# Moving one query projection ahead of the attention stage, shifting a pair of heads, and splitting norms into smaller steps in a one-core encoder layer

## The chip, the cores and the metric

One core of a Trainium2 chip runs the whole program. The metric is the device time of one execution in microseconds (us), smaller is better, as the median of several runs. Engines are named as in the profile: PE is TensorE's matmuls, PEld its weight loads, DVE is VectorE, ACT is ScalarE, POOL is GpSimd, SP is SyncE, which issues the DMAs.

## The reference, cut to what matters

One encoder layer over 1024 prompt frames and 32 sample frames of width 1024, all in float32:

```python
h = adaln_in(x, gains[0], sh1, sc1)
x = x + FFN_RES * g1[:, None] * rmsnorm(swiglu(h, w1_gate, w1_up, w1_down), gains[1])
h = adaln_in(x, gains[2], sh2, sc2)
qa, ka, va, qb, kb, vb = jnp.split(h @ w_in, SPLITS, axis=-1)
oa, ob, rows = mixers(qa, ka, va, qb, kb, vb)
o = jnp.concatenate([rmsnorm(oa, group_gains[:WIDTH_A]), rmsnorm(ob, group_gains[WIDTH_A:])], axis=-1) @ w_out
x = x + g2[:, None] * rmsnorm(o, gains[3])
h = adaln_in(x, gains[4], sh3, sc3)
x = x + FFN_RES * g3[:, None] * rmsnorm(swiglu(h, w2_gate, w2_up, w2_down), gains[5])
```

Mixer A is chunked attention with 8 heads over up to 576 keys; mixer B has 8 query heads on 2 key heads, a window of 128, and a learned sink per head. Both have relative biases. The new key and value rows are outputs too.

## The kernel before

**Tiling.** Activations lie transposed (features on the partitions), in three blocks of frames, `TB`: 384, 384 and 288 wide, the last one holding the 32 sample frames. A product with a weight is kept exact to float32 by splitting both sides into a high and a low part: `mm3` (L324 to L327) does three matmuls for each of the 8 slices k of the features: weight high times input high, weight high times input low, weight low times input high. `split_w` (L299) loads one weight column block of 512 KB by a DMA into a `raw` tile (3 buffers), rounds it on ACT into the high part (L303) and subtracts on DVE for the low part (L304), in a tile of `wpool` (8 buffers).

**Stages.** The first feed-forward part (`ffn` with key h1), then projections and attention, then the output product `wo` with its norms, then the second feed-forward part (key h3). Norms run aside: `step(n)` advances the generators in the list `side`, first one first. A norm squares and sums on ACT, POOL and DVE, takes the sums of the partitions by PE (`pss`, L357), computes the root on a dozen small DVE operations (L334 to L338), spreads it by PE (`pr`, L405), and scales: `norm_h` writes `h_hi` (ACT, L440 or L444) and `h_lo` (DVE or POOL, L446, L449). Between sums and spread `mean_rstd` lets `waits[0]` steps pass.

**Around the attention.** For each block tb the loop at L1077 waits for the block's norm (`need(("h2", tb))`), then projects mixer B's keys and values (`kv_piece`, tile `pv`), the queries of mixer B's first pair (`q0_piece`, tile `pq`), and mixer A's first values. Then 72 attention tiles n run: 36 of mixer B (four pairs of one sample tile and 8 tiles i each), 18 of mixer A's pairs 0 and 1, and from n = 54 on those of pairs 2 and 3, sorted by i + LAG * (p - 2). Each tile is scores (`S`, `Sb`, `Ss`), softmax on DVE and ACT, transposes (`pp`, `ppb`, `pps`), and products with the values (`po`).

**Fill.** The projections that later tiles need run between the tiles. `STAGES` says from which tile to which a list of units is spread; `fill(rate)` takes from it, twice a tile, what the costs in `COST` allow. `prepare` gets a pair's bias and cached keys three tiles ahead. From n = 67 on one piece of the output product (`out_piece`, tile `wo`, 24 matmuls) goes in per tile; the other 19 follow the loop, with six steps of the norms behind each. `group_norm(tb, g)` norms one block of mixer A (g = 0) or B (g = 1) ahead of them.

**Order.** What is written is a priority. When the program is built, a list scheduler with its own timeline picks for each engine, among the instructions whose inputs and buffers it believes ready, the one that is written first. On the chip each engine then runs its list in that order. Some projections are seen between the last `dn` matmuls of the feed-forward part for that reason.

The parameters that the change touches: OUTSTEP, STAGES, LAG, and the order of the matmuls in `up` inside `ffn` (L540).

Of the kernel before, what the change touches and what calls it, by code (L numbers as in the profile page):

```python
# [8 lines left out]
F32R = mybir.dt.float32r  # L9
# [8 lines left out]
KT = D // 128  # L18
# [16 lines left out]

PACE = 2
FAST = 10
OUTSTEP = 6
ABREAST = 1
POOL_ADDS = (1, 2)  # L40
GN1 = 55
# [21 lines left out]
LEAD_B = 2  # L63
MANUAL = False
WAIT = 3
PREP = 3
STAGES = ((0, 34), (37, 54))
RATE = 1.0
OUTS = (0,) * 13 + (1,) * 5
LAG = 0.5  # L70
KEEP = [(5, 6, 7), None, None]


# [1 line left out]
def encoder_step(ctx: ExitStack, tc, x_prompt, x_sample, cache_a_k, cache_a_v, cache_b_k, cache_b_v,  # L75
# [220 lines left out]
        return bs  # L296


    def split_w(src):  # L299
        r = rpool.tile([128, 8, 128], F32, name="raw", tag="r")  # L300
        dma.dma_start(r, src)
        w = wpool.tile([128, 2, 8, 128], F32R, name="w", tag="w")
        ae.activation(w[:, 0], r, AF.Copy)  # L303
        ve.tensor_sub(w[:, 1], r, w[:, 0])  # L304
        return w

    def split_cols(wm, c):
        return split_w(wm[0, :, 128 * c:128 * c + 128].rearrange("(k p) n -> p k n", p=128))

    def split_rows(wm, r):  # L310
        return split_w(wm[0, 128 * r:128 * r + 128, :].rearrange("p (k n) -> p k n", n=128))
# [12 lines left out]
    def mm3(ps, w, k, hi, lo, start, stop):  # L324
        te.matmul(ps, w[:, 0, k], hi, start=start, stop=False)  # L325
        te.matmul(ps, w[:, 0, k], lo, start=False, stop=False)  # L326
        te.matmul(ps, w[:, 1, k], hi, start=False, stop=stop)  # L327


    def rsqrt(v, n, m):  # L330
# [170 lines left out]
    def need(key):  # L501
        while key not in done:
            step(1)
# [21 lines left out]
    def ffn(key, H, F, wg, wu, wd, per_group, key_out, after, beside=lambda ff, tb: None):  # L525
# [10 lines left out]
        for r, (gi, blocks) in enumerate(plan):  # L536
# [3 lines left out]
            def up(ff, tb):  # L540
                need((key, tb))
                w = TB[tb][1]
                hi, lo = H[tb]
                ps = [p1("gate"), p1("up")]
                for s in range(2):
                    for k in range(KT):
                        mm3(ps[s][:, :w], wgu[ff][s], k, hi[:, k, :], lo[:, k, :], k == 0, k == KT - 1)
                    step(FAST if gi == 0 else PACE)
                sl = s_tile([128, 384], "sl")
                ae.activation(sl[:, :w], ps[0][:, :w], AF.Silu)  # L550
                ve.tensor_tensor(sl[:, :w], sl[:, :w], ps[1][:, :w], op=OP.mult)  # L551
                g = g_tile([128, 2, 384], "gg", F32R)
                ae.activation(g[:, 0, :w], sl[:, :w], AF.Copy)
                ve.tensor_sub(g[:, 1, :w], sl[:, :w], g[:, 0, :w])  # L554
                gs[ff, tb] = g
                beside(ff, tb)
                if late:
                    late.pop()()
# [516 lines left out]
        dma.dma_start(nbv_s[0, 0].rearrange("t h d -> t (h d)"), kvbs[:, 128:256])  # L1075

    for tb in range(3):  # L1077
        need(("h2", tb))
        if tb == 0:
            keys_cached()  # L1080
        for x in token_tiles(tb):
            run(kv_piece(*x))
        if tb == 2:
            KSB = wpool.tile([128, 2, 1024], F32R, name="KSB", tag="w")
            if PRIME:
                primed.append(load_qb(1))
            keys = [lambda: keys_new(0, 4), lambda: keys_new(4, 4), keys_sample]
        if tb == 2 and KEARLY == 1:
            keys.pop(0)()
        run(q0_piece(tb))  # L1090
        for i, x in enumerate(token_tiles(tb)):
            run(v0_piece(*x))
            if tb == 2 and KEARLY:
                keys and keys.pop(0)()
# [27 lines left out]
    def unit_qb(p):  # L1122
        return [(("B", p), lambda: load_qb(p), lambda w: flow_qb(p, w))]

    def unit_va(g):
        return [(("V", g), lambda: load_va(g), lambda w: flow_va(g, w))]

    def unit_qka(p):
        return [(("K", p), lambda: load_ka(p), lambda w: flow_ka(p, w)),
                (("A", p), lambda: load_qa(p), lambda w: flow_qa(p, w))]  # L1130

    flows = [(*STAGES[0], unit_qb(1) + unit_qb(2) + unit_qb(3) + unit_va(1) + unit_qka(0)),
             (*STAGES[1], unit_qka(1) + unit_qka(2) + unit_qka(3))]
    COST = {"B": 10.6, "V": 23.4, "K": 10.6, "A": 10.6}

# [28 lines left out]
    def out_piece():  # L1164
        tb, m = outs.pop(0)
        need(("gn", tb, 1))
        need(("gn", tb, 0))
        w = TB[tb][1]
        hi, lo = OH[tb]
        if F2[tb] is None:  # L1170
            F2[tb] = u_tile(tb, "fo", F32)
        if m not in wo:
            load_wo(m)
        ps = p1("wo")
        for k in range(KT):
            mm3(ps[:, :w], wo[m], k, hi[:, k, :], lo[:, k, :], k == 0, k == KT - 1)
        ae.activation(F2[tb][:, m, :], ps[:, :w], AF.Copy)
        if KEEP[tb] is not None and m not in KEEP[tb]:
            del wo[m]
        if outs and outs[0][0] != tb:  # L1180
            begin(("h3", tb), between(F2[tb], tb, 1, H3))
# [32 lines left out]

        return LEAD_B if t < 36 else 1

    ready.add(("B", 0))
    todo = []
    for t in range(N):
        at = max(-1, t - lead(t))  # L1220
# [12 lines left out]
    with tc.manual_schedule(engines={mybir.EngineType.PE}) if MANUAL else ExitStack():  # L1233
        waits[0] = WAIT
        preps += [prepare(*key) for key in opens[0]]
        scores(-1, 1)
        if PRIME == 2:
            now = flow(flows[0][2])
            fill(PFILL)
        for n in range(N):  # L1240
# [11 lines left out]
                if outs and n >= whole[outs[0][0]] + 2:  # L1252
                    out_piece()
            for key in opens.get(n + PREP, []):
                while key not in ready:
                    budget -= next(now, 0)
                preps.append(prepare(*key))
            for half in range(2):
# [10 lines left out]
                    budget = 0.0  # L1269
    tiles[N - 1].av()  # L1270
    begin(("gn", 2, 0), group_norm(2, 0), first=True)
    while outs:
        out_piece()
        step(OUTSTEP)
    begin(("h3", 2), between(F2[2], 2, 1, H3))


# [78 lines left out]
```

## Time and profile before

| | us |
|---|---|
| median of 3 runs | 2217.93 (2214.45 to 2221.46) |
| the profiled execution's own time | 2217.6 |
| its span, first to last instruction | 2215.8 |
| PE busy in the span | 2161.6 (98%) |
| PEld busy | 2068.6 (93%) |
| DVE busy | 1239.1 (56%) |
| ACT busy | 697.8 (31%) |
| POOL busy | 179.2 (8%) |
| mean granted clock of TensorE | 0.984 |

The span runs from 0 to 2215.8 us: loading and the first norms to about 75 us, the first feed-forward part to about 850, projections to 917, mixer B to about 1065, mixer A to 1327, the output product to 1414, and the second feed-forward part to the end. The page's row of PE's busy tenths is 9 in nearly all of 40 slices; the exceptions are at the start, at the end, and in some slices from 885 to 1450 us. The row of the granted clock has its lower digits in the same places.

### The profile page before, as it was taken

What the parts mean: (1) busy time and instruction counts of PE and PEld (TensorE: products, weight loads), DVE (VectorE), ACT (ScalarE), POOL (GpSimd) and SP (SyncE); (2) the same over time, 40 slices, a digit from 0 to 9 for tenths busy, and PEclk for the clock granted to TensorE, in tenths of its full rate; (3) what the DMA queues carried; (4) which work ended last, traced back from release to release, by engine and by line L of the source; (5) the groups of instructions that cost most, each with busy time, mean ns of one, the idle gap of its engine ahead of it and who ended that gap; (6) DMA issues with size and microseconds to landing.
All of it is one profiled execution on the core that took longest, in us unless ns stands there. A gap on an engine that the chain in (4) does not pass through costs nothing.

```text
span 2215.8 us, 33976 instructions
## 1 busy us (share of the span) xinstructions
PE 2161.6 (98%) x14012; PEld 2068.6 (93%) x14012; DVE 1239.1 (56%) x2425; ACT 697.8 (31%) x1450; POOL 179.2 (8%) x281
## 2 busy tenths in 40 slices
PE   6999999999999999899999899999999999999998
PEld 4999999999999999799787589999999999999998
DVE  5788667874333497677444865785333333333336
ACT  4411111111121253576444663542111111111133
POOL 1100000000000023001110313220000000000000
PEclk8999999999999999899999899999999999999999
DMA  9253334434122352111112121424211111111122
GB/s 323 93 153 118 111 96 124 143 101 129 39 66 69 101 184 93 38 39 30 50 30 62 46 77 67 134 86 120 66 58 39 57 39 39 58 38 58 39 69 79
DMA packets 200623, 186.03 MB, mean 84 GB/s; under 512 B 7597, under 2 KB 169813, under 8 KB 199317
## 3 DMA queue, kind: packets, MB, share of 16 engines
q1 hardware_dynamic: 200468, 183.87, 27.1%
q8 instruction: 110, 1.80, 0.3%
q14 instruction: 45, 0.36, 0.1%
HBM read 164.12 MB, written 22.86 MB: 84 GB/s over the span
## 4 chain that ended last, share of the span: by engine, by line
PE 90%; DVE 4%; DMA 3%; ACT 1%; issue 1%; POOL 0%; SPq 0%; ACTq 0%; DVEq 0%; POOLq 0%
PE dn L325 7%; PE dn L326 7%; PE dn L327 7%; PE gate L327 7%; PE gate L326 7%; PE up L327 7%; PE up L326 7%; PE gate L325 7%; PE up L325 7%; PE po L713 3%; PE S L752 2%; PE pq L325 2%; PE pq L327 2%; PE pq L326 2%; DMA raw<-in_w_gate_dram 1%; PE pp L776 1%
## 5 line engine op out<-in xcount | busy, mean ns | idle before, releaser
L326 PE MATMUL gate<-h_lo,w 128*128 128x384 f32 (+1 forms) x1056 | 340.2, 322 | 4.0 <-DVE h_lo L446 4.0
L325 PE MATMUL dn<-gg,w 128*128 128x384 f32 (+1 forms) x1056 | 341.4, 325 | 1.1 <-DVE facc L581 1.0
L581 DVE TENSOR_TENSOR facc<-dn,facc 128x768 f32<-128x768 f32 (+1 forms) x240 | 212.9, 889 | 230.2 <-PE dn L327 229.9
L326 PE MATMUL dn<-gg,w 128*128 128x384 f32 (+1 forms) x1056 | 340.6, 323 | 0.6 <-DVE gg L554 0.6
L325 PE MATMUL gate<-h_hi,w 128*128 128x384 f32 (+1 forms) x1056 | 341.0, 323 | 0.0
L327 PE MATMUL gate<-h_hi,w 128*128 128x384 f32 (+1 forms) x1056 | 340.4, 322 | 0.0
L325 PE MATMUL up<-h_hi,w 128*128 128x384 f32 (+1 forms) x1056 | 340.2, 322 | 0.0
L326 PE MATMUL up<-h_lo,w 128*128 128x384 f32 (+1 forms) x1056 | 340.0, 322 | 0.0
L327 PE MATMUL dn<-gg,w 128*128 128x384 f32 (+1 forms) x1056 | 340.0, 322 | 0.0
L327 PE MATMUL up<-h_hi,w 128*128 128x384 f32 (+1 forms) x1056 | 339.9, 322 | 0.0
L304 DVE TENSOR_TENSOR w<-raw,w 128x1024 fp32r<-128x1024 f32 x187 | 231.5, 1246 | 150.5 <-ACT w L303 150.3
L303 ACT ACTIVATE w<-raw 128x1024 fp32r<-128x1024 f32 x187 | 195.7, 1056 | 266.1 <-PE dn L327 103.5
L550 ACT ACTIVATE sl<-gate 128x384 f32<-128x384 f32 (+1 forms) x132 | 60.9, 462 | 563.9 <-PE gate L327 560.9
L551 DVE TENSOR_TENSOR sl<-sl,up 128x384 f32<-128x384 f32 (+1 forms) x132 | 68.5, 519 | 292.1 <-PE up L327 286.1
L326 PEld LDWEIGHTS gate<-h_lo,w 128*128 128x128 f32 x1056 | 198.6, 188 | 4.6 <-DVE h_lo L446 4.6
L325 PEld LDWEIGHTS dn<-gg,w 128*128 128x128 f32 x1056 | 199.2, 189 | 1.6 <-DVE facc L581 1.2
L326 PEld LDWEIGHTS dn<-gg,w 128*128 128x128 f32 x1056 | 199.2, 189 | 1.0 <-DVE gg L554 0.9
L327 PEld LDWEIGHTS dn<-gg,w 128*128 128x128 f32 x1056 | 199.1, 189 | 0.0
L325 PEld LDWEIGHTS gate<-h_hi,w 128*128 128x128 f32 x1056 | 198.7, 188 | 0.1
L327 PEld LDWEIGHTS gate<-h_hi,w 128*128 128x128 f32 x1056 | 198.7, 188 | 0.0
L327 PEld LDWEIGHTS up<-h_hi,w 128*128 128x128 f32 x1056 | 198.7, 188 | 0.0
L325 PEld LDWEIGHTS up<-h_hi,w 128*128 128x128 f32 x1056 | 198.5, 188 | 0.0
(224 smaller groups left out, 3367.4 us busy)
## 6 DMA issues: line engine op xcount, KB each, us to landing
raw<-in_w_mod_dram SPq DMA_DIRECT2D x56, 512.0 KB, 4.0
raw<-in_w_gate_dram SPq DMA_DIRECT2D x54, 512.0 KB, 4.0
raw<-in_w_up_dram SPq DMA_DIRECT2D x54, 512.0 KB, 4.7
raw<-in_w_down_dram SPq DMA_DIRECT2D x54, 512.0 KB, 4.5
raw<-in_w_in_dram SPq DMA_DIRECT2D x18, 512.0 KB, 4.3
wm<-in_w_mod_dram SPq DMA_DIRECT2D x8, 1024.0 KB, 7.4
raw<-in_w_out_dram SPq DMA_DIRECT2D x13, 512.0 KB, 4.5
xr<-xs SPq DMA_DIRECT2D x16, 384.0 KB, 3.5
```

The costliest lines, as they stand in the source:

```text
L303: ae.activation(w[:, 0], r, AF.Copy)
L304: ve.tensor_sub(w[:, 1], r, w[:, 0])
L325: te.matmul(ps, w[:, 0, k], hi, start=start, stop=False)
L326: te.matmul(ps, w[:, 0, k], lo, start=False, stop=False)
L327: te.matmul(ps, w[:, 1, k], hi, start=False, stop=stop)
L550: ae.activation(sl[:, :w], ps[0][:, :w], AF.Silu)
L551: ve.tensor_tensor(sl[:, :w], sl[:, :w], ps[1][:, :w], op=OP.mult)
L581: ve.tensor_tensor(o, ps[:, :, :w], o, op=OP.add)
L713: te.matmul(po[64 * h:64 * h + 64, :n], vsl(j, h, kn), PT(h, j, kn), start=j == 0, stop=j == nt - 1)
L752: te.matmul(S[:, c:ce], self.T[:, h, :], KQ[:, 0, 128 * k0 + c:128 * k0 + ce], start=True, stop=True)
L776: te.transpose(pp[:, j - j0, :], P[:, 128 * j:128 * j + 128], ident)
```

## The change

It does six things. The queries of mixer B's second pair are no longer a unit of the fill: their weights are split into a tile of `upool` under the tag `u`, the products of the blocks 0 and 1 are written ahead of the wait for the last block's norm, with two steps behind each half, and that of block 2 behind the first scores. Pair 3 of mixer A lags pair 2 by 2.5 tiles and not 0.5, so that its sample tile is n = 57 and not 55; all else that hangs on the position of the tiles moves with it, as the start of the norms of blocks 0 and 1 (n = 65 and 71, before 63 and 69). The second fill runs from n = 34 to 57, before 37 to 54. `prepare` may start when a pair's keys are there, before its queries. In `up` the 16 matmuls with the input's high part come first and the 8 with its low part last (`mm_all`). An output piece takes two steps after each quarter, before six behind the whole; in the pieces behind the loop five steps pass between sums and spread, before three.

```diff
-OUTSTEP = 6
+OUTSTEP = 2
+OUTWAIT = 5
-STAGES = ((0, 34), (37, 54))
+STAGES = ((0, 34), (34, 57))
-LAG = 0.5
+LAG = 2.5
...
-    def split_w(src):
+    def split_w(src, pool=None):
...
+            w = pool.tile([128, 2, 8, 128], F32R, name="wu", tag="u", bufs=6)
...
+    def mm_all(ps, w, hi, lo):
+        for k in range(KT):
+            te.matmul(ps, w[:, 0, k], hi[:, k, :], start=k == 0, stop=False)
+            te.matmul(ps, w[:, 1, k], hi[:, k, :], start=False, stop=False)
+        for k in range(KT):
+            te.matmul(ps, w[:, 0, k], lo[:, k, :], start=False, stop=k == KT - 1)
...
-                    for k in range(KT):
-                        mm3(ps[s][:, :w], wgu[ff][s], k, hi[:, k, :], lo[:, k, :], k == 0, k == KT - 1)
+                    mm_all(ps[s][:, :w], wgu[ff][s], hi, lo)
...
     for tb in range(3):
+        if tb == 2:
+            q1_piece = start_qb(1, split_cols(w_in, 13, upool))
+            for b in range(2):
+                for _ in q1_piece(b):
+                    step(2)
         need(("h2", tb))
...
-    flows = [(*STAGES[0], unit_qb(1) + unit_qb(2) + unit_qb(3) + unit_va(1) + unit_qka(0)),
+    flows = [(*STAGES[0], unit_qb(2) + unit_qb(3) + unit_va(1) + unit_qka(0)),
...
             mm3(ps[:, :w], wo[m], k, hi[:, k, :], lo[:, k, :], k == 0, k == KT - 1)
+            if k % 2 and k < KT - 1:
+                step(OUTSTEP)
...
-    ready.add(("B", 0))
+    ready |= {("B", 0), ("B", 1)}
...
         scores(-1, 1)
+        run(q1_piece(2))
...
-                while key not in ready:
+                while key not in ready and ("K", key[1]) not in ready:
...
+    waits[0] = OUTWAIT
     while outs:
         out_piece()
         step(OUTSTEP)
+    waits[0] = WAIT
```

## Rows read from the trace of the kernel before

**Rows 1.** The page: the span, and busy time, share and instructions of PE and PEld.

```profile
span 2215.8 us, 33976 instructions
...
PE 2161.6 (98%) x14012; PEld 2068.6 (93%) x14012; DVE 1239.1 (56%) x2425; ACT 697.8 (31%) x1450; POOL 179.2 (8%) x281
```

**Rows 2.** Timeline of PE, 885 to 896 us: start, us, instruction, [idle before <-releaser].

```profile
888.24 1.75 PE L405 MATMUL pr<-ident,ry 128*128 128x128 f32 x6 [2.44 <-DVE ry L338]
...
891.11 0.58 PE L669 MATMUL pv<-w,h_hi 128*128 128x256 f32 x1 [1.11 <-ACT h_hi L444]
...
894.66 1.08 PE L1057 MATMUL pk<-ident,vt 128*128 128x128 f32 x4 [1.91 <-DVE n L420]
```

**Rows 3.** Busy time by stretch: length, busy us (instructions) per engine, granted clock, DMA.

```profile
885.64:895.40 9.76, 4.29 (x19) 3.41 (x19) 7.28 (x32) 4.79 (x15) 0.31 (x1) 0.58 0.00 0
...
895.40:897.50 2.10, 2.10 (x12) 1.97 (x11) 2.04 (x7) 2.06 (x8) 1.58 (x4) 0.50 0.00 0
```

**Rows 4.** The same for one tile alone (PE, PEld, DVE or ACT): `up`, then `pq`.

```profile
1419.04:1423.20 4.16, 4.16 (x24) 4.00 (x24) 0.00 (x0) 1.00 0.45 137
...
904.19:907.39 3.20, 3.20 (x24) 3.12 (x24) 0.00 (x0) 1.00 0.11 31
```

**Rows 5.** The page's groups of the weight split: busy us, mean ns, idle before.

```profile
L304 DVE TENSOR_TENSOR w<-raw,w 128x1024 fp32r<-128x1024 f32 x187 | 231.5, 1246 | 150.5 <-ACT w L303 150.3
...
L303 ACT ACTIVATE w<-raw 128x1024 fp32r<-128x1024 f32 x187 | 195.7, 1056 | 266.1 <-PE dn L327 103.5
```

**Rows 6.** Timeline of DVE, 872 to 896 us.

```profile
874.61 4.49 DVE L464 SCALAR_TENSOR_TENSOR facc<-facc,gcoef,pr 128x256 f32<-128x256 f32 x16 [5.69 <-PE pr L405]
```

**Rows 7.** Timeline of PE, 915 to 925 us.

```profile
920.53 0.39 PE L813 MATMUL Sb<-KSB,qs 128*128 128x256 f32 x1 [2.38 <-ACT Ps L888]
```

**Rows 8.** Busy time by stretch, from mixer B's start to the second feed-forward part.

```profile
921.40:924.80 3.40, 3.40 (x13) 2.98 (x14) 3.34 (x11) 1.91 (x7) 0.23 (x1) 0.50 0.03 10
...
1062.58:1071.65 9.07, 4.87 (x39) 2.99 (x39) 4.82 (x14) 6.03 (x18) 3.89 (x10) 1.00 0.85 235
...
1212.10:1256.00 43.90, 37.56 (x219) 22.92 (x219) 34.13 (x95) 30.02 (x79) 19.14 (x51) 0.81 0.33 93
...
1225.20:1235.40 10.20, 10.20 (x47) 6.59 (x47) 8.06 (x31) 5.95 (x21) 5.33 (x14) 0.50 0.36 107
...
1242.20:1249.10 6.90, 6.53 (x19) 3.28 (x21) 4.63 (x13) 4.41 (x12) 3.46 (x9) 0.51 0.00 1
...
1334.40:1341.20 6.80, 5.19 (x17) 4.93 (x18) 4.17 (x14) 2.16 (x4) 1.20 (x1) 0.50 0.01 2
...
1443.60:1447.00 3.40, 3.40 (x12) 3.40 (x11) 3.40 (x5) 0.68 (x1) 2.09 (x3) 0.50 0.02 5
```

**Rows 9.** Timeline of PE, 1332 to 1338 us.

```profile
1332.89 0.76 PE L357 MATMUL pss<-ones,sq 128*128 128x1 f32 x6 [0.58 <-POOL sq L370]
...
1336.01 1.76 PE L405 MATMUL pr<-ident,ry 128*128 128x128 f32 x6 [2.36 <-DVE ry L338]
...
1337.70 0.69 PE L325 MATMUL wo<-o_hi,w 128*128 128x384 f32 x1
```

**Rows 10.** Timeline of PE and ACT, where the feed-forward parts wait for low parts.

```profile
74.07 0.45 PE L326 MATMUL gate<-h_lo,w 128*128 128x384 f32 x1 [1.83 <-DVE h_lo L446]
...
1442.92 0.45 PE L326 MATMUL gate<-h_lo,w 128*128 128x384 f32 x1 [2.13 <-DVE h_lo L446]
...
1438.15 2.72 ACT L444 ACTIVATE h_hi<-n,modT 128x384 fp32r<-128x384 f32 x5 [2.24 <-DVE n L420]
```

**Rows 11.** Busy time by stretch: mixer B, mixer A's first pairs, its later pairs.

```profile
930.00:1050.00 120.00, 119.48 (x959) 108.70 (x957) 91.73 (x325) 82.68 (x289) 9.78 (x34) 1.00 0.11 32
...
1090.00:1200.00 110.00, 109.86 (x724) 89.84 (x723) 48.04 (x121) 48.01 (x121) 9.52 (x36) 1.00 0.10 28
...
1212.00:1327.00 115.00, 108.00 (x723) 78.59 (x722) 86.48 (x230) 80.47 (x179) 33.34 (x73) 0.93 0.24 69
```

**Rows 12.** Waits of PE in the whole run: waited for, us in total, times, longest.

```profile
PE pr L405 <- DVE ry L338: 4.8, 2, 2.4
```

More of the change, by code (lines that the diff above doesn't have):

```diff
@@ L296, in bias_tiles @@
         return bs
-    def split_w(src):
+    def split_w(src, pool=None):
         r = rpool.tile([128, 8, 128], F32, name="raw", tag="r")
         dma.dma_start(r, src)
-        w = wpool.tile([128, 2, 8, 128], F32R, name="w", tag="w")
+        if pool is None:
+            w = wpool.tile([128, 2, 8, 128], F32R, name="w", tag="w")
+        else:
+            w = pool.tile([128, 2, 8, 128], F32R, name="wu", tag="u", bufs=6)
         ae.activation(w[:, 0], r, AF.Copy)
@@ L305, in split_w, with split_cols @@
         return w
-    def split_cols(wm, c):
-        return split_w(wm[0, :, 128 * c:128 * c + 128].rearrange("(k p) n -> p k n", p=128))
+    def split_cols(wm, c, pool=None):
+        return split_w(wm[0, :, 128 * c:128 * c + 128].rearrange("(k p) n -> p k n", p=128), pool)
     def split_rows(wm, r):
```

## The prediction, made before the changed kernel was run

> **What bounds the kernel now.** Read first the page's busy line: PE is busy 2161.6 of 2215.8 us, and each of its 14012 matmuls has a weight load of its own [rows 1]. The change removes no matmul, load or DMA, so it can give back only two things: time in which PE stands still (54.2 us in all), and time in which it works at the lower of its two clocks (1.2 GHz, a granted clock of 0.50) after standing still. Nearly none of either falls in the body of the two feed-forward parts; both lie in a few places between 885 and 1447 us, and at the start and end. Read next PE's timeline for what ended each idle stretch [rows 2, 7, 9, 10], then the stretches by granted clock [rows 3, 8]: a stretch of 3.40 us at 0.50 in which PE is busy throughout costs 1.7 us, since the same work takes half of it at 2.4 GHz. Of the 3.40-us kind there are five after 70 us, at 74.9, 921.4, 1071.6, 1433.4 and 1443.6, each behind a short wait; two are shown [rows 8].
>
> A rule of the Trainium skill bears on this reading: Perfetto Trace Analysis, Identifying the Most-Contended Engine, says that matmul busy time is a poor measure of headroom and the weight loads' share a better one. In 1212.10 to 1256.00 PE looks 86% busy but PEld is busy 22.92 of 43.90 us, against 89.84 of 110.00 with fill between the tiles [rows 8, 11]. By busy time 6.3 us are to be had there; by the weight loads, an estimate, 43.90 - 22.92/0.817 = 15.8. The clock's rows below come to 14.7, so the trace sides with the rule.
>
> **The price of a projection.** 24 matmuls on 384 columns take 4.16 us at full clock, on 288 columns 3.20 [rows 4]. One query projection is 2 x 4.16 + 3.20 = 11.5 us.
>
> **Part 1, queries ahead of the last norm.** PE's last sums end at 885.64; then it waits for the root, for `h_hi` and for the last scaled pair [rows 2]. In the 9.76 us to 895.40 it does 16 small matmuls of the kernel (6 `pr`, 6 `pv`, 4 `pk`; three more records overlap the ends), none longer than the 0.133 us of a 288-column one [rows 3, 4], 2.1 us together. So 7.6 us are lost, and half of the next 2.10, at 0.50: 8.7. The change puts two blocks, 8.3 us of matmuls whose inputs were ready long before, at this place. Gain 8.3. It needs the weights in time. Their DMA moves ahead on SP, one of 512 KB as before, past nothing that the norm needs; the split takes 1.06 us of ACT and 1.25 of DVE [rows 5], and DVE stands 5.69 us idle before 874.61 [rows 6]. That idle time hides it; if it is gone, the last norm ends up to 2.3 us later, and PE is covered to 893.9, while the first high part came at about 891 [rows 2]. So it costs nothing. The weights' place is a `u` buffer, free once block 1's residual has been read; at this point four of six hold the normed blocks 0 and 1.
>
> **Part 2, block 2 of these queries.** 3.20 us behind the first scores, where the second scores wait 2.38 us for an exponential [rows 7], with 3.40 us at 0.50 behind it [rows 8]. Gain 2.38 + 1.7 = 4.1.
>
> **Part 3, fill from n = 34.** Six projections, 69 us, were spread over 17 tiles (4.06 each) and are now spread over 23 (3.0 each): 9.0 us move to the tiles 34 to 36, and 9.0 to 54 to 56. From 1062.58 to 1071.65, PE idles 9.07 - 4.87 = 4.2 us while mixer B runs out and mixer A's first keys are prepared [rows 8]; a 3.40-us stretch at 0.50 follows, the pattern of the row at 921.40. At most 5.9; 9.0 us of work is enough, but its first weights need a `wpool` buffer that mixer B gives back only about there. Taken: 4.2, from 0 to 5.9.
>
> **Part 4, the later pairs.** 1212.10 to 1256.00 idles 6.3 us, and 10.20 + 6.53 busy us lie at 0.50 [rows 8], 8.4 lost: 14.7. Two sample tiles and two short tiles of pairs 2 and 3 came in a row, with three group norms beside them. Now 9.0 us of fill and longer tiles lie between. I take half, 8; from 0 to 14.7.
>
> **Part 5, quarter steps.** At 1332.89 and 1336.01 PE waits 0.58 + 2.36 us, since the spread `pr` was listed right behind the sums and `wo` matmuls stood behind it [rows 9]; half of 5.19 us at 0.50 follows [rows 8]. Together 5.5. With five steps between, and two per quarter piece, 2.5 quarters of 1.04 us, 2.6 us, lie between sums and spread. Sums to spread took 3.12. Taken: 4.5.
>
> **Part 6, high parts first.** Twice PE waits for the first low part, 1.83 and 2.13 us, with 3.40 us at 0.50 behind each [rows 10, 8]: 3.5 + 3.8 = 7.3. Five high parts were written by 1440.87 [rows 10]; each now feeds two matmuls in `gate` and two in `up`, 20 x 0.173 = 3.5 us of work for a gap of 2.13. Each matmul has its own weight load already [rows 1], so the order costs no loads. Taken: 7. The edit of `prepare` and the list of ready units move only when things are written; nothing.
>
> **What is paid.** (a) Mixer B loses 11.5 us of fill. PE is busy 119.48 of 120 us there, DVE 91.73, ACT 82.68, PEld 108.70 [rows 11]. If matmuls set the pace, all 11.5 come off; if each tile's chain through DVE and ACT does, none. DVE at 76% goes to about 83%, if the some 140 us from 921 to 1063 lose 11.5: nearer to the first. Loss 4, from 0 to 11.5. (b) Mixer A's first pairs lose 18.0 us of fill; DVE is busy 48.04 of 110 [rows 11], so PE sets the pace. Loss 3, from 0 to 18.0. (c) Tiles and norms in a new order make waits of their own that the trace can't show. The nearest rows are 2.36 or 2.38 us with 1.7 of clock behind; none to two of these, 0 to 8.2. Below nothing is open too, since norms that move on sooner could end the 0.62-us kind of wait, but no row prices it. Taken: 3.
>
> **The sum.** 8.3 + 4.1 + 4.2 + 8 + 4.5 + 7 = 36.1 given back, 10 paid: 26. The profiled execution took 2217.6, its span and 1.8 around it; the median, 2217.93, is 0.3 above. 2217.6 - 26.1 = 2191.5, and with the 0.3 about 2192.
>
> **Rivals.** *The fill was hidden anyway* (the tiles' chains set the pace). Then (a) is 11.5, which gives 2199, and with (b) at 18.0 too 2214; middle 2206. For it: PEld's share falls to 82% in mixer A's first pairs. Against: PE shows hardly an idle gap there. 0.18.
>
> *Spread waits in the quarter pieces, slower.* PE runs its list in order, so each `pr` now stands between quarters of a `wo` piece and holds them until DVE's root chain is through. Where that chain finds DVE busy with a weight split (1.25) or a residual, each spread waits up to 2.4 us and 1.7 of clock follow: 4.1. Eight norms run from n = 65 to the second feed-forward part (four group norms, and two each for the blocks 0 and 1). Without parts 4's and 5's gain of 12.5, the rest gives 13.6; four waits are worth more than that, so from four of eight on it is slower, and all eight give 2217.9 - 13.6 + 32.8 = 2237; six, 2229. Against: in the whole run only two spreads wait, with the same chain [rows 12]. 0.05.
>
> A rule of the skill stands behind this rival: TensorE: Matmul & The Clock Gate, What overlaps and what doesn't, has matmuls start and end in program order. The trace agrees: 48 `wo` matmuls that needed nothing began at 1337.70, only behind the `pr` at 1336.01 [rows 9].
>
> *The early queries come late.* If the `u` buffer or the split is late, parts 1 and 2 fall away: 26.1 - 12.4 = 13.7, 2204. Against: rows 6 and the four of six buffers. 0.07.
>
> *All of it covered.* Parts 3 to 6 at their ceilings, (a) to (c) at a quarter: 8.3 + 4.1 + 5.9 + 14.7 + 5.5 + 7.3 = 45.8, less 2.5, gives 2175. 0.06.
>
> **How the numbers follow.** The forecast has 0.64: 2192, its own range 2182 to 2202. The range for 8 in 10 takes in late queries and most of the first rival above it, and the forecast with nothing paid (2217.9 - 36.1 = 2182) and a part of the last case below: 2179 to 2209. About 0.3%, 6.7 us, is what a measurement of this kernel can tell from no change: faster is below 2211.3, slower above 2224.6. Forecast, late queries, full cover and nearly all of the first rival are faster: 0.64 + 0.07 + 0.06 + 0.11 = 0.88. Same takes the rest of the first rival and the slower one at four or five waits: 0.07 + 0.01 = 0.08. Slower: 0.04.
>
> **What would show it.** Part 1: 48 `pq` matmuls at full clock where 885.64 to 895.40 was, and no stretch at 0.50 there. Part 2: no wait at the second scores. Part 3: `pq` between the last `ppb` and the first `pps`. Part 4: fewer us at 0.50 in the 44 us behind the later pairs' first sample tile. Part 5: no `pr` with over 1 us idle before it. Part 6: no `gate` waiting for `h_lo`. Costs: mixer B's 34 tiles should take some 7.5 us less than before, its first pairs of A some 15. Wrong would be: the same tile times with thinner fill, or new `pr` and `S` waits of 2 us and more.

## The result: 0.2% slower, and the profile after

The changed kernel took 2220.25 us (median; 2216.84 to 2223.63), the kernel before, run beside it, 2214.81. The ratio is 1.0023, 95% interval 1.0016 to 1.003: 5.1 us more, where 26 less were forecast. Below, a ratio times 2216 is given as us against before (+5.1 here), with the 95% interval of the ratio in brackets.

PE does the same work in nearly the same time. The page of after (span, then busy time, share and instructions per engine), against rows 1:

```profile
span 2217.4 us, 33983 instructions
...
PE 2157.8 (97%) x14012; PEld 2066.8 (93%) x14012; DVE 1237.5 (56%) x2425; ACT 695.7 (31%) x1450; POOL 180.2 (8%) x281
```

PE is 3.8 us less busy, but stands still for 59.6 us where it stood still for 54.2. To see where, cut both spans at the same five events: last `dn` of the first feed-forward part, first `Ss` of mixer B, first `Ss` of mixer A, first `Ss` of A's third pair, last `wo`. Columns as in rows 3. First before, then after:

```profile
849.59:916.64 67.05, 61.58 (x472) 59.59 (x470) 42.29 (x112) 31.40 (x73) 14.51 (x18) 0.92 0.19 59
916.64:1066.94 150.30, 144.73 (x1139) 130.48 (x1138) 110.87 (x395) 103.77 (x362) 12.36 (x44) 0.99 0.13 36
1066.94:1212.11 145.17, 143.46 (x955) 117.53 (x955) 66.30 (x162) 65.04 (x167) 16.62 (x56) 0.99 0.13 37
1212.11:1414.04 201.93, 191.77 (x1253) 160.69 (x1252) 142.36 (x343) 116.46 (x239) 63.24 (x93) 0.94 0.25 78
1414.04:2215.76 801.72, 790.97 (x4977) 787.37 (x4975) 343.03 (x532) 177.83 (x293) 28.71 (x28) 0.99 0.21 63
```

```profile
848.63:921.94 73.31, 69.61 (x521) 67.86 (x519) 42.84 (x111) 32.03 (x75) 14.76 (x18) 0.95 0.21 65
921.94:1071.57 149.63, 143.54 (x1115) 128.05 (x1114) 110.58 (x397) 104.64 (x362) 12.26 (x44) 0.98 0.15 42
1071.57:1199.01 127.44, 127.44 (x862) 101.51 (x860) 63.52 (x162) 62.13 (x162) 15.41 (x56) 1.00 0.11 29
1199.01:1422.37 223.36, 202.80 (x1330) 175.30 (x1330) 146.13 (x349) 116.11 (x242) 66.82 (x95) 0.94 0.24 73
1422.37:2217.43 795.06, 786.45 (x4971) 782.61 (x4969) 339.76 (x526) 177.58 (x293) 27.25 (x27) 1.00 0.21 63
```

The two traces differ by only 1.6 us, since the one of before is of an execution 2.8 us above that kernel's median and the one of after 0.8 below its own; so 3.5 of the 5.1 us lie in no stretch. Single executions of before lie up to 10 us apart, so a difference of a microsecond or two between two traces shows nothing by itself.

The terms of the sum, laid on these five stretches and what comes ahead of them, against what came (part 6 with 3.5 and 3.8, of which the sum took 7):

| stretch | forecast (terms) | measured |
|---|---|---|
| up to the last `dn` | -3.5 (part 6, first place) | -1.0 |
| projections | 0 (8.3 of work comes in, 8.3 of waits go) | +6.3 |
| mixer B and its end | -3.6 (-8.3 of part 1, -4.1 of part 2, +9.0 of fill and -4.2 of part 3, +4 of (a)) | -0.7 |
| mixer A, first pairs | -15 (-18 of fill, +3 of (b)) | -17.7 |
| mixer A, later pairs and output | -0.5 (+9 of fill, -8 of part 4, -4.5 of part 5, +3 of (c)) | +21.4 |
| second feed-forward part | -3.8 (part 6, second place) | -6.7 |

How the fill moved is seen from `pq` alone in those stretches (PE, PEld, ACT): the first pairs of mixer A before, then first pairs and later pairs after.

```profile
1066.94:1212.11 145.17, 79.45 (x432) 69.84 (x432) 8.70 (x24) 0.99 0.13 37
```

```profile
1071.57:1199.01 127.44, 65.40 (x336) 53.45 (x336) 6.77 (x19) 1.00 0.11 29
1199.01:1422.37 223.36, 14.54 (x72) 12.63 (x72) 1.45 (x4) 0.94 0.24 73
```

A whole projection, 72 matmuls or 11.5 us by rows 4, went into the later pairs. Of their 21.4 us, 9.9 are therefore loss, where a gain of 9.5 was forecast. PE stood still there for 223.36 - 202.80 = 20.6 us; before, it was 10.2. Its timeline in after names the longest waits, the last two of which answer rows 9:

```profile
1217.37 0.83 PE L369 MATMUL pss<-ones,sq 128*128 128x1 f32 x6 [1.95 <-POOL sq L382]
...
1229.46 0.91 PE L763 MATMUL S<-KQ,qz 128*128 128x384 f32 x2 [1.82 <-ACT Ps L899]
...
1284.83 0.69 PE L329 MATMUL wo<-o_hi,w 128*128 128x384 f32 x1 [3.46 <-ACT o_hi L1170]
...
1329.68 0.93 PE L417 MATMUL pr<-ident,ry 128*128 128x128 f32 x6 [2.82 <-DVE ry L350]
...
1342.49 0.76 PE L369 MATMUL pss<-ones,sq 128*128 128x1 f32 x6 [2.99 <-POOL sq L382]
...
1345.53 1.78 PE L417 MATMUL pr<-ident,ry 128*128 128x128 f32 x6 [2.27 <-DVE ry L350]
1347.24 0.69 PE L329 MATMUL wo<-o_hi,w 128*128 128x384 f32 x1
```

Every wait but the second is a step of a norm: its sums, its spread, or the normed input of an output piece. The last two are one norm, that of the last block's mixer A, for which before waits 0.58 and 2.36 us (rows 9). Work for them is there: six output pieces have run by then, and the other two of block 0, 48 `wo` matmuls that do not need this norm, stand in PE's list behind its spread and begin at 1347.24. It is so before, too, at 1337.70.

At the last norm ahead of mixer B, PE (first fence) and DVE (second) of after, against rows 2:

```profile
887.86 1.34 PE L369 MATMUL pss<-ones,sq 128*128 128x1 f32 x12
...
893.23 0.94 PE L417 MATMUL pr<-ident,ry 128*128 128x128 f32 x6
...
895.29 0.39 PE L680 MATMUL pv<-w,h_hi 128*128 128x256 f32 x1 [1.11 <-ACT h_hi L456]
...
898.85 1.09 PE L1068 MATMUL pk<-ident,vt 128*128 128x128 f32 x4 [2.59 <-DVE n L432]
```

```profile
884.79 0.46 DVE L382 TENSOR_TENSOR sq<-sq 128x288 f32<-128x288 f32 x1
889.24 0.16 DVE L400 TENSOR_SCALAR rv<-pss 128x2 f32<-128x2 f32 x1 [3.99 <-PE pss L369]
```

The squares are summed at 885.25 (884.79 + 0.46), 0.6 us later than before, but PE's sums begin at 887.86: 25 early `pq` matmuls stand ahead of them in PE's list, and 23 more ahead of the spread. DVE idles 3.99 us over it. The first `pv` of the last block comes at 895.29, before at 891.11. The waits of 1.11 and 1.91 us are still there, 4.2 us later, as 1.11 and 2.59, and half-speed work still follows them (rows 3 for before):

```profile
885.64:895.40 9.76, 8.65 (x56) 8.36 (x55) 3.10 (x17) 1.66 (x4) 0.31 (x1) 1.00 0.00 0
...
897.40:904.20 6.80, 5.35 (x25) 5.12 (x26) 6.64 (x24) 5.79 (x19) 3.00 (x6) 0.50 0.01 2
```

The high parts did what they should at both places of rows 10: no `gate` waits for `h_lo`, and the clock stays up. But a wait of PE at 52.08 is longer in after, 2.49 us where before has 0.26:

```profile
73.50:79.00 5.50, 5.50 (x34) 5.50 (x33) 5.50 (x8) 3.93 (x9) 2.03 (x2) 1.00 0.01 3
1422.50:1456.00 33.50, 32.90 (x200) 32.23 (x199) 25.60 (x47) 16.71 (x27) 9.63 (x8) 1.00 0.41 129
```

```profile
52.08 1.94 PE L628 MATMUL pt<-ident,X 128*128 128x128 f32 x16 [2.49 <-DMA X<-in_x_prompt_dram]
```

### The profile page after: what moved, and what is told of

It reads as the page before. It is cut to its first block, busy times and chain, and to the rows that moved or that the text cites. A ratio compares the mean times of both kernels' runs of the same rounds, so it can differ in the third digit from the quotient of the medians.

```text
span 2217.4 us, 33983 instructions
## 1 busy us (share of the span) xinstructions
PE 2157.8 (97%) x14012; PEld 2066.8 (93%) x14012; DVE 1237.5 (56%) x2425; ACT 695.7 (31%) x1450; POOL 180.2 (8%) x281
## 4 chain that ended last, share of the span: by engine, by line
PE 89%; DVE 6%; DMA 3%; ACT 1%; issue 1%; SPq 0%; POOL 0%; ACTq 0%; DVEq 0%; POOLq 0%
PE up L339 7%; PE up L336 7%; PE gate L339 7%; PE dn L329 7%; PE dn L330 7%; PE dn L331 7%; PE up L337 7%; PE gate L336 7%; PE gate L337 7%; PE po L724 2%; PE S L763 2%; PE pq L329 2%; PE pq L331 2%; PE pq L330 2%; PE pp L787 1%
## 5 line engine op out<-in xcount | busy, mean ns | idle before, releaser
L336 PE MATMUL up<-h_hi,w 128*128 128x384 f32 (+1 forms) x1056 | 331.8, 323 | 0.0
L336 PE MATMUL gate<-h_hi,w 128*128 128x384 f32 (+1 forms) x1056 | 331.4, 322 | 0.0
L337 PE MATMUL up<-h_hi,w 128*128 128x384 f32 (+1 forms) x1056 | 331.0, 321 | 0.0
L337 PE MATMUL gate<-h_hi,w 128*128 128x384 f32 (+1 forms) x1056 | 330.3, 321 | 0.0
L339 PE MATMUL gate<-h_lo,w 128*128 128x384 f32 (+1 forms) x1056 | 196.3, 321 | 0.0
L339 PE MATMUL up<-h_lo,w 128*128 128x384 f32 (+1 forms) x1056 | 193.0, 321 | 0.0
L380 POOL TENSOR_TENSOR sq<-sq 128x384 f32<-128x384 f32 (+1 forms) x48 | 52.1, 1095 | 1519.3 <-ACT sq L376 854.2
```

Source lines behind the costliest of these rows:

```text
L336: te.matmul(ps, w[:, 0, k], hi[:, k, :], start=k == 0, stop=False)
L337: te.matmul(ps, w[:, 1, k], hi[:, k, :], start=False, stop=False)
L339: te.matmul(ps, w[:, 0, k], lo[:, k, :], start=False, stop=k == KT - 1)
L380: e.tensor_tensor(sq[:, 0, :w], sq[:, 0, :w], sq[:, 1, :w], op=OP.add)
```

## The experiments

Each was timed against before on the same chip. Unless a diff says otherwise, a kernel is before plus what is named.

### Part by part

**e1_early**: parts 1 and 2 alone (the first hunks of the diff ahead of the prediction, with `run(q1_piece(2))`).

> Part 1 and 2 alone on the kernel before. Theory Q (the last norm's sums and spread stand in PE's list behind the early matmuls, so the norm itself ends some 4 us later, and mixer B's tiles do not speed up by the whole 11.5 us taken from them): the time lies within 2 us of the kernel before, and the first `pv` of the last block comes about 4 us later than before. Theory P (the prediction's terms 8.3 + 4.1 - 4 hold, and what was lost was lost elsewhere): 7 to 9 us faster.

Measured: 1.0004 (0.9995 to 1.0014), +0.9 us. Of the 12.4 us of parts 1 and 2, less 4 for (a), nothing is left: the projections take 73.25 us, 6.2 more than before, and mixer B, first to last score, 5.5 less. The first `pv` of the last block comes at 895.00, as late as in after, which is what the theory of the queue asks for: the norm is late because its own two steps on PE are.

**e2_high**: part 6 alone (`mm_all`).

> Only the order of the matmuls in the gate and up products (high parts first). If the two waits for low parts are all it ends: 6 to 7 us faster. If their end only brings the next wait forward (the low parts come at DVE's pace): 2 to 4 us faster.

Measured: 0.9981 (0.9971 to 0.9991), -4.2 us of 7 forecast. From the last `wo` to the end the trace has 3.66 us less than before, which is the second place of rows 10 (forecast 3.8). The first place gave nothing: PE now waits 2.65 us at 52.20, at a `pt` that before waited 0.26; of `gate`, `up` and `dn` 47 have started by 60 us, before 62, and by 200 us 874, before 875. The other traces bear this out: up to the last `dn` the ten kernels without part 6 take 847.9 to 849.8 us, the nine with it 848.2 to 851.7; that `pt` waits at most 1.54 us without it and 2.49 to 3.19 with it, but for two of the nine that have no wait there. So a wait at another place goes with the end of the one at 74.07. What makes it is open: this trace names ACT's `h_hi` as its releaser, that of after the DMA of `X`.

**e3_lag**: part 4 alone.

```diff
-LAG = 0.5
+LAG = 2.5
```

> Only pair 3 of mixer A shifted by two more tiles; the second fill stays at tiles 37 to 54. Theory L (the shift is what made the change lose: norms of blocks 0 and 1 start two tiles later against the first output pieces, and the end of the loop waits for them): 6 to 12 us slower than before. Rival F (the lengthening of the late pairs' stage is only the fill that was moved into it): within 3 us of before, or faster.

Measured: 1.0065 (1.005 to 1.008), +14.4 us, where part 4 was to give 8. Its later pairs and output take 218.38 us against 201.93, and PE idles 218.38 - 197.30 = 21.1 us in them:

```profile
1212.98:1431.36 218.38, 197.30 (x1258) 166.60 (x1258) 145.45 (x350) 114.94 (x239) 63.70 (x95) 0.91 0.24 75
```

Its timeline of PE has the last norm's pair of waits, as after has it:

```profile
1291.34 0.69 PE L776 MATMUL pp<-ident,P 128*128 128x128 f32 x4 [3.39 <-ACT PT L705]
...
1341.79 0.76 PE L357 MATMUL pss<-ones,sq 128*128 128x1 f32 x6 [3.19 <-POOL sq L370]
...
1344.82 1.79 PE L405 MATMUL pr<-ident,ry 128*128 128x128 f32 x6 [2.27 <-DVE ry L338]
...
1361.52 1.33 PE L325 MATMUL wo<-o_hi,w 128*128 128x384 f32 x3 [3.51 <-ACT o_hi L1154]
```

The pair is 5.46 us where before has 2.94. The wait behind it is new: the first output piece of block 1 stands still until its norm is done, at a place where block 0's eight pieces are used up.

**e4_fill**: part 3 and the edit of `prepare`, without the shift.

```diff
-STAGES = ((0, 34), (37, 54))
+STAGES = ((0, 34), (34, 54))
...
-                while key not in ready:
+                while key not in ready and ("K", key[1]) not in ready:
```

> Only the second fill begun at tile 34 and not 37, ending at 54 as before, with the earlier preparation of a pair. Prediction's part 3: 4 us faster (0 to 6). Rival: the gap between mixer B and A stays, since the first weights come late, and the same matmuls are only done earlier: within 2 us.

Measured: 0.9988 (0.9979 to 0.9998), -2.7 us, of 4.2 forecast (0 to 5.9). From mixer B's first score to A's third pair PE idles 3.7 us in its trace, before 7.3, and the 3.4 us at 0.50 at 1071.6 are gone; the later pairs and output idle 2.3 us more.

**e5_quarter**: part 5 alone.

> Only the quarter steps in the output pieces, and five steps between sums and spread behind the loop. Part 5 of the prediction: 4 to 5 us faster, with no spread waiting over 1 us behind the loop. The sum of the parts run alone so far is 0.9 - 4.2 + 14.4 - 2.7 = 8.4 us slower, and the whole change 5.1 us slower, so if the parts add up, this one is about 3 us faster. Rival: within 1 us, since the spread and the next piece are put in the same order as before.

Measured: 1.0066 (1.0053 to 1.0079), +14.6 us, where part 5 was to give 4.5. One spread waits 5.22 us. PE's timeline there, then DVE's:

```profile
1313.64 0.73 PE L358 MATMUL pss<-ones,sq 128*128 128x1 f32 x6
...
1322.54 1.65 PE L406 MATMUL pr<-ident,ry 128*128 128x128 f32 x6 [5.22 <-DVE ry L339]
```

```profile
1314.91 1.21 DVE L305 TENSOR_TENSOR w<-raw,w 128x1024 fp32r<-128x1024 f32 x1
...
1316.23 0.15 DVE L392 TENSOR_SCALAR rv<-pss 128x3 f32<-128x3 f32 x1
...
1319.60 1.22 DVE L305 TENSOR_TENSOR w<-raw,w 128x1024 fp32r<-128x1024 f32 x1
...
1320.80 1.22 DVE L305 TENSOR_TENSOR w<-raw,w 128x1024 fp32r<-128x1024 f32 x1
...
1322.32 0.16 DVE L339 SCALAR_TENSOR_TENSOR ry<-rt,ry 128x3 f32<-128x3 f32 x1
```

The root's dozen short operations take 6.2 us (1316.23 to 1322.48), since two weight splits and the softmax of other tiles lie between them, and a third split ahead of them; on a free DVE they take 2.2 (1343.29 to 1345.47 in after, from the row of `ry` that ends the wait at 1345.53). Between these sums and this spread PE's list has four score matmuls and no `wo`; before, 24 `wo` matmuls lay between the sums at 1316.61 and the spread at 1325.28.

### Why the shift costs: where the norms begin

**e6_normlate**: no tile moves; only the norms of blocks 0 and 1 begin two tiles later, at n = 65 and 71, as the shift makes them.

```diff
-                if n == whole[tb] + 2:
+                if n == whole[tb] + 4:
```

> The kernel before, its tiles in their old order, but the norms of mixer A's output for the blocks 0 and 1 begin two tiles later (n = 65 and 71, as the shift makes them). Theory N (the shift costs because these norms come closer to the output pieces that need them): the wait of PE for `o_hi` behind the loop is there as with the shift, and the time is 6 to 14 us above before. Rival T (the order of the tiles itself costs, by its bursts on DVE and ACT): within 3 us of before.

Measured: 1.0093 (1.0077 to 1.0108), +20.6 us, more than the shift itself. Its timeline of PE has the sums of the same pair, and the wait for block 1's norm behind it, as e3_lag:

```profile
1293.49 2.47 PE L752 MATMUL S<-KQ,qz 128*128 128x512 f32 x4 [4.97 <-ACT P L761]
...
1345.25 0.76 PE L357 MATMUL pss<-ones,sq 128*128 128x1 f32 x6 [3.19 <-POOL sq L370]
...
1365.03 1.33 PE L325 MATMUL wo<-o_hi,w 128*128 128x384 f32 x3 [3.51 <-ACT o_hi L1154]
```

PE idles 24.8 us in the later pairs and output, before 10.2, and 37.5 us of them are at 0.50, before 23.9. So the start of the norms is enough to make the loss, with the tiles in their old order; what the order does by itself was not measured.

**e12_norm_early**: e9_high_fill (below) with the norms one tile earlier than before, `whole[tb] + 1`.

> The kernel of e9_high_fill (2210.4 us), with the norms behind mixer A of the first two blocks begun one tile earlier (1 tile after the block is whole, not 2). Theory of the norm's start: beginning them two tiles later cost 19.4 us in e6_normlate, so one tile earlier is worth something too if any wait is left there: 2 to 6 us, 2204 to 2208. Rival: at 2 tiles the waits are already gone or are set by something else, and the time is that of e9_high_fill within 1.5 us. It could even lose, if the norm's first sums then wait in TensorE's list for their squares: 2213 or more.

Measured: 0.999 (0.9979 to 1.0), 2214.02 us, -2.2 us, 4 more than e9_high_fill, whose interval it touches. There is no gain. The last branch of the expectation, that it loses because the sums then wait for their squares, has the time and a wait that fits: the sums at 1335.61 wait 4.09 us, in e9_high_fill the same sums, at 1330.0, do not wait. But from the first `Ss` of mixer B to the end its trace is only 1.1 us longer than that of e9_high_fill, so the loss is not shown.

### Why the quarter steps cost: sums to spread

**e7_quarter_behind**: quarter steps only in the pieces behind the loop.

```diff
-            if k % 2 and k < KT - 1:
+            if behind and k % 2 and k < KT - 1:
                 step(OUTSTEP)
```

> Quarter steps only in the pieces behind the loop; the five pieces between the tiles keep no steps inside. Theory S (inside the loop the six extra steps a piece shorten the time between a norm's sums and its spread, so that the spread stands in PE's list ahead of what DVE can have ready: 5.22 us idle before one spread with quarter steps everywhere): that wait is gone, and the time is between 4 us faster than before and 2 us slower. Rival E (the steps behind the loop are what costs): still over 8 us slower than before.

Measured: 1.0006 (0.9997 to 1.0014), +1.3 us: the loss is in the pieces inside the loop. But the place for which part 5 was counted, behind the loop, gives nothing either. The view of all waits shows it, against rows 12 (4.8 us, 2 times):

```profile
PE pr L406 <- DVE ry L339: 7.2, 3, 2.4
```

The sums at 1332.92 are followed by their spread at 1336.05, 2.37 us of it a wait, with no `wo` matmul between, as before, and 48 stand behind. The quarters that part 5 wanted there are not in PE's list at that place.

**e8_quarter_spaced**: quarter steps everywhere, but nine steps between sums and spread from n = 67 on.

```diff
+            if n == 67:
+                waits[0] = 9
```

> Quarter steps everywhere, but from tile 67 on nine steps and not three pass between a norm's sums and its spread. Theory S: the 5.22 us wait at the spread goes, with 3 to 7 us at the lower clock behind it; 5 to 9 us less than with quarter steps alone (13.6 us above before), so 4 to 9 above before. Rival: the norm begun early takes DVE and ACT from the tiles whatever the spacing; within 3 us of quarter steps alone.

Measured: 1.0024 (1.0014 to 1.0035), +5.3 us, 9.3 less than e5_quarter. The spread that waited 5.22 us there has no wait here. It is as far behind its sums (8.70 us, there 8.90), but the way is filled, with 24 `wo` matmuls among others:

```profile
1317.44 0.72 PE L358 MATMUL pss<-ones,sq 128*128 128x1 f32 x6
...
1326.14 0.93 PE L406 MATMUL pr<-ident,ry 128*128 128x128 f32 x6
```

The last norm's pair of waits stays: 3.19 us at 1345.42 and 2.37 at 1348.99.

### Why the early queries give nothing

**e10_early_behind**: e1_early with the first early block queued behind the last norm's sums and the second behind its spread.

```diff
+            while len(side) > 0:
+                step(1)
             for b in range(2):
-                for _ in q1_piece(b):
-                    step(2)
+                with tc.issue_after(mark[("pss", "pr")[b]].ins):
+                    run(q1_piece(b))
```

> The early queries alone, as in e1_early (2217.3 us, 1.1 us above before), but the first block's 24 matmuls are queued behind the last block's sums and the second block's 24 behind its spread. Theory of the delayed norm: the sums run some 3.4 us earlier again, the first pv of the last block comes back from 895.0 us to about 891.5 to 893, and the time is 2 to 4 us below e1_early, about 2213.5 to 2215.5. Theory of mixer B's own pace: the norm is earlier but the end of mixer B comes no earlier, and the time is within 1.5 us of e1_early.

Measured: 0.9982 (0.9972 to 0.9993), -4.0 us, 4.9 less than e1_early. Sums and spread come 3.7 and 1.6 us earlier than in e1_early, and the wait at the first `pv` is gone:

```profile
883.88 1.63 PE L360 MATMUL pss<-ones,sq 128*128 128x1 f32 x12 [0.79 <-POOL sq L373]
...
891.31 0.94 PE L409 MATMUL pr<-ident,ry 128*128 128x128 f32 x6
```

The stretch of the projections takes 69.85 us, in e1_early 73.25, so of the 8.3 us moved in, 5.5 are now hidden (67.05 + 8.3 - 69.85), before the repair 2.1:

```profile
848.03:917.88 69.85, 68.91 (x521) 67.35 (x519) 42.91 (x111) 31.61 (x75) 14.20 (x18) 0.98 0.22 68
```

**u_early_behind**: the whole change with that repair and nothing else.

> The whole change, with the one repair of e10_early_behind: the first block's early matmuls behind the last norm's sums, the second block's behind its spread. If the delayed norm costs the whole change what it costs the early queries alone (5 us in ratio), and the rest is independent of it, the time is about 5 us below the whole change: 2215, level with before. If the new order behind it (the tail of mixer A) eats it again, it stays at about 2220.

Measured: 1.0 (0.9991 to 1.0009). 5.1 us come back in company, 4.9 alone.

**e11_thin**: the other half of the price, mixer B. 54 `pq` matmuls are left out of it and put nowhere, so that those queries are partial sums (36 of 384 columns and 18 of 288, 8.6 us by rows 4; the expectation counts 48 of the former).

```diff
-        return qk_proj(w, qt, qs, 0.125)
+        return qk_proj(w, qt, qs, 0.125, 2 if p == 1 else KT)
```

> The kernel before, with the queries of mixer B's second pair projected over 2 of the 8 slices of the contraction: 18 of 24 matmuls are left out in each of the three blocks, so that the result of those queries is a partial sum. About 54 matmuls, some 9 us of TensorE time (48 of 384 columns at 3.20/24 us, 18 of the narrow block at about 0.12 us: 8.5 us), are gone from mixer B and nothing is moved into another stage. If the matmuls set mixer B's pace, its stretch from the first to the last tile (142.9 us) is 8 to 9 us shorter and so is the whole, about 2207. If the tiles' chains set it, the stretch is 1 to 4 us shorter and the whole is 2212 to 2215.

Measured: 0.9996 (0.9986 to 1.0006), -0.9 us. The 8.6 us of matmuls gone from mixer B give nothing that can be told from 0. What took their place is seen in its first 28.97 us, in before and then in e11_thin:

```profile
916.64:945.61 28.97, 26.55 (x177) 23.73 (x177) 21.09 (x75) 18.66 (x66) 1.54 (x5) 0.94 0.07 21
```

```profile
918.08:947.05 28.97, 24.38 (x142) 20.33 (x141) 21.38 (x83) 21.25 (x75) 1.54 (x5) 0.76 0.07 21
```

35 matmuls fewer, 2.2 us more idle time, and the granted clock falls from 0.94 to 0.76. If all that lies under 1.00 is time at 0.50, that is 13.9 us at 1.2 GHz against 3.5, so up to 5.2 us lost at half speed. In the traces of ten other kernels whose mixer B begins with the same code, 3.4 to 6.8 us there are at 0.50, so 3.5 us lost are the least. Neither theory had the clock in it.

### In company

**u_noshift**: the whole change without the shift (LAG 0.5, second fill to n = 54).

> The whole change with the shift taken back: LAG 0.5, and the second fill from 34 to 54. If the shift is what made the change lose, and its cost is the same in this company as alone (14.4 us): 2220.3 - 14.4, some 9 to 10 us faster than before. If the cost depends on the rest: between before and 5 us faster.

Measured: 1.006 (1.0047 to 1.0072), +13.3 us, where its parts alone add up to 8.6. The expectation was missed: without the shift the change is worse, not better, as the quarter steps then cost what they cost alone (a `pr` with 6.21 us idle before it, at 1323.37).

**c_high_quarter_fill**: parts 3, 5 and 6 (fill to n = 54).

> The parts that alone were faster or not yet seen, together: high parts first, quarter steps, the second fill from 34 to 54; neither the early queries nor the shift. If parts add up: 4.2 + 2.7 + about 3, so 10 us faster than before, a little faster than the change without the shift.

Measured: 1.005 (1.0036 to 1.0064), +11.1 us, where its parts alone add up to 7.7; missed as well: e9_high_fill, the same without the quarter steps, is at -6.2.

**u_noquarter**: the whole change without part 5.

> The whole change without the quarter steps: shift, early queries, high parts and fill stay. If parts add up: 0.9 - 4.2 + 14.4 - 2.7, 8.4 us slower than before, 3 us above the whole change. If the shift and the quarter steps each cost alone and cancel in company (the shift starts the norms later, the inner steps move them on faster): 5 us or more above the whole change. If not: at or below the whole change.

Measured: 1.0034 (1.0022 to 1.0046), +7.5 us, where its parts alone add up to 8.4; its interval overlaps that of the whole change. So the quarter steps, +14.6 alone, cost nothing on top of the shift. The traces show a trade of waits: this one has e3_lag's wait of 3.51 us for `o_hi` (at 1353.93), which the whole change lacks, and lacks the spread that waits 2.82 us there (at 1329.68). Why the quarter steps move that norm so was not taken apart.

**e9_high_fill**: parts 3 and 6 alone.

> High parts first and the second fill from 34 to 54 alone, without quarter steps, shift or early queries. If these two add up: 4.2 + 2.7, so 7 us faster than before (ratio 0.997). If the order of the tail is upset by any change of what runs ahead of it: slower than before.

Measured: 0.9972 (0.9963 to 0.9982), -6.2 us; the two alone sum to -6.9. These add.

**e13_high_early_behind**: e9_high_fill with the early queries in the order of e10_early_behind.

> The kernel of e9_high_fill (high parts first and the fill from tile 34) with the ordered early queries of e10_early_behind added. If the parts add up, it stands below e9_high_fill (2210.4 us) by what e10_early_behind stands below before: by the theory of the delayed norm 1 to 3 us, 2207.5 to 2209.5; by the theory of mixer B's own pace it is 0 to 2 us above e9_high_fill.

Measured: 0.9947 (0.9932 to 0.9963), 2203.68 us, -11.7 us: the best kernel of this study. The sum of its parts, -10.2, lies inside its interval, so no more than adding up is shown; it is 4 us below the expectation's lower end, as e10_early_behind alone was worth 4 and not 1 to 3. Its later pairs and output take 200.51 us with the clock at 0.97, in e9_high_fill 207.39 at 0.94, and the sums that wait 1.82 us there (at 1344.49) wait 0.25:

```profile
1204.09:1404.60 200.51, 190.01 (x1276) 161.46 (x1276) 141.88 (x343) 115.22 (x241) 62.14 (x93) 0.97 0.26 78
```

Why that norm falls better there was not taken apart.

## Why the prediction was wrong

It said 2192, range 2179 to 2209, with 0.88 for faster; it came to 0.23% slower, inside "same" (0.08). The reading of the waits before was right in the main: each place named did lose time, though the 3.4 us at 0.50 at 74.9 are missing in eight of the nine other traces of kernels without part 6. What failed is what the edits would put there.

- **Parts 1 and 2, less (a): 8.4 forecast, nothing measured (+0.9, e1_early), 4.0 with the order repaired (e10_early_behind).** The step that failed is "8.3 us of matmuls whose inputs were ready long before, at this place". They were so ready that they stood ahead of the norm's sums and spread, and the norm that they were to cover came 4.2 us later. Only SP, ACT and DVE were asked whether the norm could be late; PE's own queue was left out. The Trainium skill, TensorE: Matmul & The Clock Gate, What overlaps and what doesn't, has matmuls in program order; the trace agrees (the sums at 887.86, their input ready at 885.25), and the prediction used the rule on part 5 and not here. The early weights were no matter, as argued: the first early `pq`, at 883.52, does not wait.
- **(a), mixer B's thinner fill: 4 taken, 6.9 measured**, if part 2 came in full. From the first to the last of its scores mixer B took 142.9 us before and 137.4 after, 5.5 us less. 8.3 us of matmuls left it, 3.2 moved within it, and the wait of rows 7 with its stretch of lower clock, 4.1, should be gone: 12.4 - 5.5 = 6.9. What came in its place are waits that before lacks: in e1_early PE waits 0.53 us at the second scores and 0.82, 0.64, 1.44 and 0.59 us at 968.5, 974.4, 1017.4 and 1019.0, with 3.4 us at 0.50 behind the last; before has one other, 0.52 us, up to the last score. The step that failed is to take PE's 119.48 busy us of 120 as a sign that matmuls nearly set the pace: busy time there doesn't say that less of it is a shorter stretch. e11_thin gives the harder form of it: taken out in one place, the matmuls leave idle time and a lower clock worth as much.
- **Part 3 (4.2): -2.7 alone**, inside its bounds, and for the reason given: the idle time between the mixers went.
- **Part 4 (8): +14.4 alone.** The step that failed is that it was costed as fill and longer tiles only. That the start of the norms moves with the tiles stands in the section on the change, but only (c) could hold what it costs; e6_normlate puts +20.6 on that start alone. The waits that this makes are spread out: in e3_lag 3.39 us at 1291, 2.5 us more than before at the last norm (1341 to 1345), whose 48 ready `wo` matmuls stand behind it, and 3.51 us at 1361, where block 0's pieces are used up and block 1's wait for their norm.
- **(b) (3): nothing.** Mixer A's first pairs ran without idle time at clock 1.00, 17.7 us shorter: 14.1 us of `pq`, 1.7 of idle time and half of 3.4 us at 0.50 went. Thinner fill, with PEld busy 80% of that stretch, is no loss there.
- **Part 5 (4.5): 0 behind the loop (e7_quarter_behind), +14.6 with the steps inside it.** The step that failed is that 2.5 quarters of a piece, 2.6 us, "lie between sums and spread": in PE's list behind the loop none does, and inside the loop the 24 `wo` that lay there before are gone. The rival of the spread waits had the mechanism, down to the weight splits; it was given 0.05 because only two spreads waited before. That is no evidence on a distance that the change itself shortens. Its count was off, though: alone, one spread more waits, 5.22 us and not up to 2.4, and in the whole change one new one, 2.82 us.
- **Part 6 (7): -4.2 alone.** The second place gave 3.7 of 3.8; the first was mis-sized, 0 of 3.5, with PE standing still at 52 us instead. Behind the last `wo` the whole change is 6.7 us shorter, 3 more than e2_high, but these need not be part 6's: the shift alone makes this stretch 5.4 us shorter (e3_lag), the quarter steps 4.1 (e5_quarter).
- **(c) (3, up to 8.2).** The norms' waits in the later pairs are what it was for, and 9.9 of loss where 9.5 of gain were forecast is far beyond its bound, because it was bounded by the waits of before and not by how far the norms could slip.

The whole is thus -6.2 (parts 3 and 6), about +1 (early queries, -4 if ordered), and what is left of 5.1, about +10, for shift and quarter steps together. u_early_behind takes back the price of the order, 5.1; e13_high_early_behind, which is that kernel without shift and quarter steps, a further 11.7.

## What to carry to other kernels

Work that is ready early covers a wait only if it is queued behind the instructions that end the wait; look at what it will stand ahead of on its own engine, above all the short steps of the chain that it is to hide. When an edit moves positions to which other things are tied (here the start of a norm), price those before the edit itself. The length of a short chain is to be measured on its engine when that is busy, not by the chain alone. And work written between two steps need not lie there in the list that is built: look where it stands before counting on it.

## What the runs showed of the hardware that was not expected

With matmuls taken out of a stretch, the rest of it ran at a lower clock: 0.94 before and 0.76 in e11_thin over the same 28.97 us (one trace of each). And a stretch at 0.50 can follow a short wait even where PE is busy nearly throughout: in e10_early_behind, behind a wait of 0.79 us, PE is busy 8.97 of 9.12 us at a mean of 0.81. It need not: the wait of `gate` at 74 us, 1.69 to 1.88 us in the ten kernels without part 6, is followed by 3.4 us at 0.50 in two of their traces and by none in eight.

```profile
883.88:893.00 9.12, 8.97 (x47) 8.71 (x48) 3.35 (x17) 0.69 (x2) 0.31 (x1) 0.81 0.08 32
```
